# Reciprocal square roots of a four-layer decoder trunk: one GpSimd power in place of ten VectorE instructions

## The chip, the cores and the metric

One core of one Trainium2 chip runs the whole kernel in a single launch. The metric is the device time of that launch in microseconds (us). The core has TensorE (PE in the profile, its weight loads PEld), VectorE (DVE), ScalarE (ACT), GpSimd (POOL) and SyncE (SP, which here only issues DMAs). Each engine works through its own instruction queue in order, and engines wait for each other by semaphores.

## The reference

The kernel computes four decoder layers over 1024 positions of width 1024, in float32. Layers 0 and 3 mix tokens with HGRN2 (a gated linear recurrence), layer 1 with sliding-window attention, layer 2 with a gated DeltaNet. Reciprocal square roots occur in every norm:

```python
def rmsnorm(x, g):
    xf = x.astype(jnp.float32)
    y = xf * lax.rsqrt(jnp.mean(xf * xf, axis=-1, keepdims=True) + EPS)
    return (y * g.astype(jnp.float32)).astype(x.dtype)

def l2norm(x):
    xf = x.astype(jnp.float32)
    return xf * lax.rsqrt(jnp.sum(xf * xf, axis=-1, keepdims=True) + EPS)

for i in range(DEPTH):                                   # DEPTH = 4
    shift, scale, gate = jnp.split(c @ ada_w[i] + ada_b[i], 3, axis=-1)
    h = rmsnorm(x, norm_g[i]) * (1.0 + scale) + shift
    kind = i % 3
    if kind == 0:   y = hgrn2_mixer(h, ...)   # o = rmsnorm(o, onorm_g) per head
    elif kind == 1: y = swa_mixer(h, ...)     # q, k = rope(rmsnorm(q), rmsnorm(k)) per head
    else:           y = gdn_mixer(h, ...)     # q, k = l2norm(q), l2norm(k); o = rmsnorm(o) per head
    x = x + gate * y
```

## The kernel before

Activations lie with the model dimension on the 128 partitions, in two halves of 512 positions. A projection is a product of float32 values split into a high and a low part, so each 128x512 step is three matmuls (`mm3`, lines 218 to 220). Weights come from HBM by SP's queue (`w_raw`), ACT rounds them to the high part (`w_hi`, line 189) and DVE subtracts to get the low part (`w_lo`, line 190).

Inside a layer, Python generators are woven together: the token mixing of one head (`mix` in HGRN2 and attention; `inverse` and `scan` in DeltaNet) is interleaved with the projections of the next head and with the conditioning (`ada`) of the next layer. The weaving gives each instruction a priority; a scheduler then fixes the order in every engine's queue before the run, by these priorities and by its own costs for the instructions. So a change of one instruction can change the order of others.

`rsqrt` (line 164) is called at 74 places, on a small tile of mean squares (4, 8 or 16 columns by 128 partitions). It guesses from the bits of the float (line 169) and makes three Newton steps of three instructions each (lines 171 to 173): ten DVE instructions, each of which needs the one before it. The calls are:

| caller | tile | columns | calls | who reads the result |
|---|---|---|---|---|
| `norm_stats`, the pre-norm at a layer's start | `n_ms` | 4 | 8 | DVE line 519, then PE line 521 (`n_rb`), on which all of the layer's input hangs |
| HGRN2 `mix`, output norm of a head's half | `hg_ms` | 4 | 32 | DVE line 1213 (or 1221 for the last head), which empties the PSUM tile `o_ps` |
| attention `ev_k` | `k_ms` | 16 | 2 | DVE line 1404 |
| attention `proj_q` | `q_ms` | 16 | 8 | DVE line 1478 and ACT line 1485, much later |
| DeltaNet `proj_kq` | `gd_ms` | 16 | 8 | DVE lines 751 to 756, then ACT |
| DeltaNet `finish` | `gd_oms` | 8 | 16 | DVE line 909, then line 913 |

POOL has little to do before the change: in DeltaNet it fills and copies small pieces (`gd_xs`, `gd_halo`, `gd_Tb`, `gd_Z`, `gd_uq`), which the causal convolution (DVE line 690) and the block inverse (DVE lines 837 and 838, PE lines 866 to 891) need; between layers it issues the DMAs that store `x` (line 142).

Of the kernel before, what the change touches and what calls it, by code (L numbers as in the profile page):

```python
# [10 lines left out]
F32 = mybir.dt.float32  # L11
F32R = mybir.dt.float32r
BF16 = mybir.dt.bfloat16
I32 = mybir.dt.int32
U8 = mybir.dt.uint8
AF = mybir.ActivationFunctionType
ALU = mybir.AluOpType
# [3 lines left out]
P = 128  # L21
# [3 lines left out]
HT = 512  # L25
NC = HT // P
EPS = 1e-6
RSQRT_MAGIC = float(0x5F3759DF)

RAW, WB = 3, 4  # L30
NB = {"n_acc": 1, "n_sq": 2}
# [50 lines left out]
class Trunk:  # L82
# [80 lines left out]

    def rsqrt(self, x, n, tag, pool=None):

        nc, pool = self.nc, pool or self.sm
        y = pool.tile([P, n], F32, name="rs_y", tag=tag + "y", bufs=2)
        t = pool.tile([P, n], F32, name="rs_t", tag=tag + "t", bufs=2)
        nc.vector.tensor_scalar(y.bitcast(I32), x.bitcast(I32), -0.5, RSQRT_MAGIC, ALU.mult, ALU.add)
        for _ in range(3):  # L170
            nc.vector.scalar_tensor_tensor(t, y, -0.5, x, ALU.mult, ALU.mult)
            nc.vector.tensor_tensor(t, t, y, ALU.mult)
            nc.vector.scalar_tensor_tensor(y, t, 1.5, y, ALU.add, ALU.mult)
        return y

    def load_w(self, src, scale=None, pool=None):
# [46 lines left out]
    def setup(self, tmp):  # L223
        nc, const, ins = self.nc, self.const, self.ins
        self.ident = const.tile([P, P], F32, name="ident")
        make_identity(nc, self.ident)
        self.ones = const.tile([P, P], F32, name="ones")
        nc.vector.memset(self.ones, 1.0)
        self.mod = const.tile([P, 4, 24], F32, name="mod")

        rows = tmp.tile([96, P], F32, name="rows")
        nc.sync.dma_start(rows[0:32, :], ins["norm_g"].rearrange("l (k p) -> (l k) p", p=P))
        nc.sync.dma_start(rows[32:64, :], ins["hgrn_lb"].rearrange("l (k p) -> (l k) p", p=P))
        nc.sync.dma_start(rows[64:72, :], ins["c"].rearrange("o (k p) -> (o k) p", p=P))
        nc.sync.dma_start(rows[72:74, :], ins["hg_onorm"])
        nc.sync.dma_start(rows[74:75, :], ins["gd_onorm"])
        brows = tmp.tile([96, P], F32, name="brows")
        nc.sync.dma_start(brows, ins["ada_b"].rearrange("l (k p) -> (l k) p", p=P))
        self.par = const.tile([P, 96], F32, name="par")
        pt = self.psum("tr", "par_ps", 1)  # L240
        nc.tensor.transpose(pt[:, :75], rows[:75, :], self.ident[:75, :75])
        nc.tensor.transpose(pt[:, 128:224], brows, self.ident[:96, :96])
        nc.vector.tensor_copy(self.par[:, :75], pt[:, :75])
        self.adab = const.tile([P, 96], F32, name="adab")
        nc.vector.tensor_copy(self.adab, pt[:, 128:224])
        self.cT = self.par[:, 64:72]
        self.gcol = const.tile([P, 4, 8], F32, name="gcol")

        lb = self.par[:, 32:64].rearrange("p (l k) -> p l k", l=4)
        m = tmp.tile([P, 8], F32, name="lb_m")  # L250
        e = tmp.tile([P, 4, 8], F32, name="lb_e")
        s = tmp.tile([P, 8], F32, name="lb_s")
        nc.vector.tensor_tensor(m, lb[:, 0, :], lb[:, 1, :], ALU.max)
        nc.vector.tensor_tensor(m, m, lb[:, 2, :], ALU.max)
        nc.vector.tensor_tensor(m, m, lb[:, 3, :], ALU.max)
        for l in range(4):
            nc.vector.tensor_tensor(e[:, l, :], lb[:, l, :], m, ALU.subtract)
        nc.scalar.activation(e, e, AF.Exp)
        nc.vector.tensor_tensor(s, e[:, 0, :], e[:, 1, :], ALU.add)
        nc.vector.tensor_tensor(s, s, e[:, 2, :], ALU.add)  # L260
        nc.vector.tensor_tensor(s, s, e[:, 3, :], ALU.add)
        nc.vector.reciprocal(s, s)
        for l in range(4):
            nc.vector.tensor_tensor(e[:, l, :], e[:, l, :], s, ALU.mult)
        self.lb = const.tile([P, 8], F32, name="lb")
        nc.vector.tensor_tensor(self.lb, e[:, 0, :], e[:, 1, :], ALU.add)
        nc.vector.tensor_tensor(self.lb, self.lb, e[:, 2, :], ALU.add)
        nc.vector.tensor_tensor(self.lb, self.lb, e[:, 3, :], ALU.add)
        nc.vector.tensor_tensor(self.lb, self.lb, e[:, 0, :], ALU.subtract)
        self.omlb = const.tile([P, 8], F32, name="omlb")  # L270
        nc.vector.tensor_scalar(self.omlb, self.lb, -1.0, 1.0, ALU.mult, ALU.add)
# [1368 lines left out]
```

## Time and profile before

| quantity | value |
|---|---|
| median of 3 runs | 2658.29 us (2656.97 to 2660.67) |
| span of the profiled execution, first to last instruction | 2664.1 us |
| busy TensorE / VectorE / ScalarE / GpSimd | 2568.7 / 2021.6 / 1323.5 / 105.7 us |
| mean granted TensorE clock | 0.990 |

The page gives the profiled execution's span but no separate total for it; the span stands 5.8 us (0.2%) above the median of the runs. Busy time of PE is the time in which at least one matmul is under way: matmuls overlap, so their durations add up to more than that. The chain of work that ended last is followed back from the last instruction; a place on it is one where the profile saw no other instruction finish later.

### The profile page before, as it was taken

Reading aid. Unit: us, or ns where it says so; the run is one execution under the profiler, and the core shown is the slowest. Engines: PE = TensorE matmul, PEld = TensorE weight load, DVE = VectorE, ACT = ScalarE, POOL = GpSimd, SP = SyncE. Lnnn points to the kernel's source line nnn. Section 1 sums busy time; section 2 is a strip of 40 time slices with the busy share of each in tenths; the row PEclk is TensorE's granted clock in tenths of the full one; section 3 lists DMA queues with packets and bytes.
Section 4 is the critical chain, followed back from the end, with each engine's and each line's share of the span. In section 5 each row is a group of like instructions: output and inputs, shape, how many; then the busy total and the mean of one; then the engine's idle time right before and its main releaser. Section 6 shows DMA issues by size and latency. Waiting matters only on the chain.

```text
span 2664.1 us, 50723 instructions
## 1 busy us (share of the span) xinstructions
PE 2568.7 (96%) x18271; PEld 2046.2 (77%) x18271; DVE 2021.6 (76%) x5655; ACT 1323.5 (50%) x3467; POOL 105.7 (4%) x278
## 2 busy tenths in 40 slices
PE   7999999999999999999999999999999999999998
PEld 4777777778888877677877777778688877787777
DVE  5585788687697877768899999988776837368675
ACT  4443444443464655545666666666544534345352
POOL 0001000001000000101000100110000000000000
PEclk8999999999999999999999999999999999999999
DMA  7333343544233253334343444333576412122343
GB/s 261 98 114 90 116 143 115 173 128 129 67 103 104 72 160 112 95 110 111 106 123 84 118 118 119 83 97 93 174 235 188 123 48 77 42 82 64 124 139 116
DMA packets 395025, 309.96 MB, mean 116 GB/s; under 512 B 74851, under 2 KB 314902, under 8 KB 394774
## 3 DMA queue, kind: packets, MB, share of 16 engines
q1 hardware_dynamic: 390550, 293.09, 37.4%
q0 software_dynamic: 4224, 13.64, 1.6%
q8 instruction: 144, 2.36, 0.4%
q14 instruction: 107, 0.88, 0.1%
HBM read 245.75 MB, written 60.88 MB: 115 GB/s over the span
## 4 chain that ended last, share of the span: by engine, by line
PE 72%; DVE 14%; DMA 6%; ACT 5%; issue 2%; SPq 1%; DVEq 0%; ACTq 0%
PE proj_ps L218 10%; PE proj_ps L220 10%; PE proj_ps L219 10%; PE outp_ps L218 4%; PE outp_ps L219 4%; PE outp_ps L220 4%; PE projw_ps L219 2%; PE projw_ps L218 2%; PE projw_ps L220 2%; DVE gd_tb L690 1%; DVE w_lo L190 1%; PE projt_ps L219 1%; PE projt_ps L220 1%; PE pv_ps L1502 1%; PE projt_ps L218 1%
## 5 line engine op out<-in xcount | busy, mean ns | idle before, releaser
L218 PE MATMUL proj_ps<-hhi,w_hi 128*128 128x512 f32 x1664 | 676.0, 407 | 3.7 <-ACT gd_tb L688 3.3
L219 PE MATMUL proj_ps<-hlo,w_hi 128*128 128x512 f32 x1664 | 671.4, 404 | 0.0
L220 PE MATMUL proj_ps<-hhi,w_lo 128*128 128x512 f32 x1664 | 671.1, 403 | 0.0
L218 PEld LDWEIGHTS proj_ps<-hhi,w_hi 128*128 128x128 f32 x1664 | 314.6, 189 | 64.3 <-ACT gd_tb L688 5.9
L220 PEld LDWEIGHTS proj_ps<-hhi,w_lo 128*128 128x128 f32 x1664 | 314.1, 189 | 58.1 <-issue 0.4
L219 PEld LDWEIGHTS proj_ps<-hlo,w_hi 128*128 128x128 f32 x1664 | 314.6, 189 | 55.2 <-issue 0.9
L189 ACT CAST w_hi<-w_raw 128x512 fp32r<-128x512 f32 x352 | 214.5, 612 | 270.5 <-PE proj_ps L219 150.8
L190 DVE TENSOR_TENSOR w_lo<-w_raw,w_hi 128x512 fp32r<-128x512 f32 x352 | 236.5, 676 | 138.2 <-ACT w_hi L189 135.2
L218 PE MATMUL outp_ps<-o_hi,w_hi 128*128 128x512 f32 x576 | 229.8, 401 | 7.9 <-ACT o_hi L1314 7.0
L219 PE MATMUL outp_ps<-o_lo,w_hi 128*128 128x512 f32 x576 | 229.6, 399 | 0.4 <-DVE o_lo L1315 0.2
L220 PE MATMUL outp_ps<-o_hi,w_lo 128*128 128x512 f32 x576 | 228.0, 398 | 0.5 <-DVE w_lo L193 0.4
L192 ACT ACTIVATE w_hi<-w_raw,par 128x512 fp32r<-128x512 f32 (+1 forms) x136 | 94.8, 698 | 131.0 <-PE outp_ps L219 88.1
L690 DVE SCALAR_TENSOR_TENSOR gd_tb<-gd_xs,taps,gd_tb 128x512 f32<-128x512 f32 x192 | 145.7, 759 | 16.2 <-ACT gd_tb L688 12.5
L218 PEld LDWEIGHTS outp_ps<-o_hi,w_hi 128*128 128x128 f32 x576 | 109.4, 190 | 31.8 <-ACT o_hi L1314 9.7
L193 DVE SCALAR_TENSOR_TENSOR w_lo<-w_raw,par,w_hi 128x512 fp32r<-128x512 f32 (+1 forms) x136 | 96.9, 715 | 45.2 <-ACT w_hi L192 43.9
L444 DVE SCALAR_TENSOR_TENSOR ada_acc<-ada_w,par,ada_acc 128x512 f32<-128x512 f32 x154 | 114.9, 746 | 19.8 <-DMA ada_w<-in_ada_w_dram 18.8
L219 PEld LDWEIGHTS outp_ps<-o_lo,w_hi 128*128 128x128 f32 x576 | 109.4, 190 | 24.9 <-DVE o_lo L1315 3.0
L220 PEld LDWEIGHTS outp_ps<-o_hi,w_lo 128*128 128x128 f32 x576 | 109.1, 190 | 22.6 <-DVE w_lo L193 1.1
L219 PE MATMUL projt_ps<-w_lo,hhi 128*128 128x256 f32 x384 | 111.6, 292 | 2.2 <-DVE w_lo L190 2.2
L218 PE MATMUL projt_ps<-w_hi,hhi 128*128 128x256 f32 x384 | 111.0, 292 | 2.7 <-ACT w_hi L189 2.7
L220 PE MATMUL projt_ps<-w_hi,hlo 128*128 128x256 f32 x384 | 111.4, 292 | 0.0
L218 PE MATMUL projw_ps<-w_hi,hhi 128*128 128x512 f32 x256 | 102.8, 407 | 2.3 <-DVE hg_q L1032 2.3
(409 smaller groups left out, 5218.0 us busy)
## 6 DMA issues: line engine op xcount, KB each, us to landing
ada_w<-in_ada_w_dram SPq DMA_DIRECT2D x160, 256.0 KB, 2.8
w_raw<-in_hg_in_w_dram SPq DMA_DIRECT2D x136, 256.0 KB, 2.9
w_raw<-in_gd_in_w_dram SPq DMA_DIRECT2D x128, 256.0 KB, 3.0
o_in<-od SPq DMA_DIRECT2D x72, 256.0 KB, 3.7
x<-xd SPq DMA_DIRECT2D x64, 256.0 KB, 4.4
w_raw<-in_gd_out_w_dram SPq DMA_DIRECT2D x64, 256.0 KB, 3.1
xd<-x POOLq DMA_DIRECT2D x48, 256.0 KB, 2.9
w_raw<-in_sw_in_w_dram SPq DMA_DIRECT2D x48, 256.0 KB, 3.1
```

What stands on the lines that cost most here:

```text
L189: nc.scalar.copy(hi, raw)
L190: nc.vector.tensor_tensor(lo, raw, hi.bitcast(F32), ALU.subtract)
L192: nc.scalar.activation(hi, raw, AF.Copy, scale=scale)
L193: nc.vector.scalar_tensor_tensor(lo, raw, scale, hi.bitcast(F32), ALU.mult, ALU.subtract)
L218: mm(out, a[0], b[0], start=start, stop=False)
L219: mm(out, a[0], b[1], start=False, stop=False)
L220: mm(out, a[1], b[0], start=False, stop=stop)
L444: self.step = self.nc.vector.scalar_tensor_tensor(acc, w, c, acc, ALU.mult, ALU.add)
L690: last = nc.vector.scalar_tensor_tensor(y, xs[:, j:j + HT], w(j), y, ALU.mult, ALU.add)
L1502: self.tied([lambda b=b, a=a: nc.tensor.matmul(po[a * 64:(a + 1) * 64], vg[:, n + 1 - nkb + b, :], p4s[b][:, :, a, :], start=b == nkb - 1, ...
```

## The change

`rsqrt` becomes one elementwise power on GpSimd: the tile of mean squares to the power of a constant tile `mhalf`, which holds -0.5 and is written once at the start. The ten DVE instructions and the scratch tile `rs_t` are gone. The line numbers shift: the power is line 166, and what stood behind `setup`'s first lines stands 5 lines earlier (line 1213 is now 1208).

```diff
@@ -25,7 +25,6 @@
-RSQRT_MAGIC = float(0x5F3759DF)
@@ -163,14 +162,8 @@
     def rsqrt(self, x, n, tag, pool=None):
 
-        nc, pool = self.nc, pool or self.sm
-        y = pool.tile([P, n], F32, name="rs_y", tag=tag + "y", bufs=2)
-        t = pool.tile([P, n], F32, name="rs_t", tag=tag + "t", bufs=2)
-        nc.vector.tensor_scalar(y.bitcast(I32), x.bitcast(I32), -0.5, RSQRT_MAGIC, ALU.mult, ALU.add)
-        for _ in range(3):
-            nc.vector.scalar_tensor_tensor(t, y, -0.5, x, ALU.mult, ALU.mult)
-            nc.vector.tensor_tensor(t, t, y, ALU.mult)
-            nc.vector.scalar_tensor_tensor(y, t, 1.5, y, ALU.add, ALU.mult)
+        y = (pool or self.sm).tile([P, n], F32, name="rs_y", tag=tag + "y", bufs=2)
+        self.nc.gpsimd.tensor_tensor(y, x, self.mhalf[:, :n], ALU.pow)
         return y
@@ -226,6 +219,8 @@
         nc.vector.memset(self.ones, 1.0)
+        self.mhalf = const.tile([P, 16], F32, name="mhalf")
+        nc.gpsimd.memset(self.mhalf, -0.5)
```

The queues after the change hold 740 DVE instructions fewer, 74 powers and one memset more on POOL, and two ACT table loads more; PE and SP hold the same instructions. The scheduler's order differs elsewhere too: some 1,095 of PE's 14,360 entries stand at another place.

VectorE in the last layer, second half of the first HGRN2 head (`hg_ssq` are the sums of squares, `hg_tmp` the normed output, `hg_f` the next head's gates). Before:

```order
L1208 TENSOR_SCALAR hg_ms<-hg_ssq 128x4
L169 TENSOR_SCALAR rs_y<-hg_ms 128x4
L171 SCALAR_TENSOR_TENSOR rs_t<-rs_y,hg_ms 128x4
L172 TENSOR_TENSOR rs_t<-rs_t,rs_y 128x4
L173 SCALAR_TENSOR_TENSOR rs_y<-rs_t,rs_y 128x4
L171 SCALAR_TENSOR_TENSOR rs_t<-rs_y,hg_ms 128x4
L172 TENSOR_TENSOR rs_t<-rs_t,rs_y 128x4
L173 SCALAR_TENSOR_TENSOR rs_y<-rs_t,rs_y 128x4
L171 SCALAR_TENSOR_TENSOR rs_t<-rs_y,hg_ms 128x4
L172 TENSOR_TENSOR rs_t<-rs_t,rs_y 128x4
L173 SCALAR_TENSOR_TENSOR rs_y<-rs_t,rs_y 128x4
L1213 TENSOR_TENSOR hg_tmp<-o_ps,rs_y 128x4x4x32
```

The same place after:

```order
L1198 SCALAR_TENSOR_TENSOR hg_S<-hg_S,hg_F,s_ps 128x128
L1203 TENSOR_SCALAR hg_ms<-hg_ssq 128x4
L1208 TENSOR_TENSOR hg_tmp<-o_ps,rs_y 128x4x4x32
L1210 STREAM_TRANSPOSE hg_tmp<-hg_tmp 128x512
L1035 TENSOR_SCALAR hg_f<-hg_f,omlb,lb 128x512
```

The reader of the result (line 1213 before, 1208 after) now stands directly behind the instruction that makes `hg_ms`, with nothing between them while the power runs on the other engine.

VectorE in DeltaNet, `finish` of the second unit's second half, where the triangular inverse (`gd_Tb`, `gd_tmp`) of the next unit runs beside it. Before:

```order
L907 TENSOR_SCALAR gd_oms<-gd_oms 128x8
L905 TENSOR_TENSOR gd_s_17368<-gd_sc 128x4
L838 TENSOR_TENSOR gd_Tb<-gd_Tb,gd_tmp 128x4x14
L169 TENSOR_SCALAR rs_y<-gd_oms 128x8
L190 TENSOR_TENSOR w_lo<-w_raw,w_hi 128x512
L837 TENSOR_TENSOR gd_tmp<-gd_A,gd_Tb 128x45
L697 SCALAR_TENSOR_TENSOR gd_q<-gd_tb 128x512
L838 TENSOR_TENSOR gd_Tb<-gd_Tb,gd_tmp 128x3x15
L171 SCALAR_TENSOR_TENSOR rs_t<-rs_y,gd_oms 128x8
L837 TENSOR_TENSOR gd_tmp<-gd_A,gd_Tb 128x30
L172 TENSOR_TENSOR rs_t<-rs_t,rs_y 128x8
```

After:

```order
L832 TENSOR_TENSOR gd_tmp<-gd_A,gd_Tb 128x56
L902 TENSOR_SCALAR gd_oms<-gd_oms 128x8
L439 SCALAR_TENSOR_TENSOR ada_acc<-ada_w,par,ada_acc 128x512
L833 TENSOR_TENSOR gd_Tb<-gd_Tb,gd_tmp 128x4x14
L904 SCALAR_TENSOR_TENSOR gd_f<-rs_y,gd_sc 128x8
L692 SCALAR_TENSOR_TENSOR gd_q<-gd_tb 128x512
```

The ten instructions were spread between others; now two instructions (lines 439 and 833) stand between `gd_oms` and the first reader of the power (line 904).

GpSimd in DeltaNet, the stretch of its queue in the same unit. Before:

```order
L680 COPY gd_xs<-gd_halo 128x3
L828 MEMSET gd_Tb 128x512
L829 MEMSET gd_Tb 64x16
L830 MEMSET gd_Tb 64x16
L678 MEMSET gd_xs 128x3
L687 COPY gd_halo<-gd_xs 128x3
```

After:

```order
L675 COPY gd_xs<-gd_halo 128x3
L166 TENSOR_TENSOR rs_y<-gd_oms,mhalf 128x8
L166 TENSOR_TENSOR rs_y<-gd_ms,mhalf 128x16
L673 MEMSET gd_xs 128x3
L823 MEMSET gd_Tb 128x512
L824 MEMSET gd_Tb 64x16
L825 MEMSET gd_Tb 64x16
L682 COPY gd_halo<-gd_xs 128x3
```

The fills and copies for the next convolution and inverse now stand behind two powers, which wait for DVE.

Over all 74 places, the number of DVE instructions between the maker of the mean squares and the first DVE reader of the power is 0 for 18 of the 32 HGRN2 calls and 1 or 2 for the other 14; at least 1 for 20 of the 24 DeltaNet calls, and at most 2; 0 to 4 for the pre-norm; 1 or 2 for `k_ms`; and 29 to 164 for `q_ms`.

## The prediction

> **What bounds the kernel now.** I read the page's totals first, then the chain of work that ended last, then TensorE's timeline, and then asked where the ten instructions stand on that chain.
>
> ```profile
> span 2664.1 us, 50723 instructions
> PE 2568.7 (96%) x18271; PEld 2046.2 (77%) x18271; DVE 2021.6 (76%) x5655; ACT 1323.5 (50%) x3467; POOL 105.7 (4%) x278
> PE 72%; DVE 14%; DMA 6%; ACT 5%; issue 2%; SPq 1%; DVEq 0%; ACTq 0%
> ```
>
> ```profile
> 2200.06 0.39 PE L219 MATMUL proj_ps<-hlo,w_hi 128*128 128x512 f32 x1
> 2200.28 0.39 PE L220 MATMUL proj_ps<-hhi,w_lo 128*128 128x512 f32 x1
> ```
>
> TensorE is busy for 2568.7 of 2664.1 us and carries 72% of the chain. Successive matmuls start 0.22 us apart, closer than one lasts: in such a stretch PE is limited by its own rate. What a relief of VectorE can win is PE's idle time, 2664.1 - 2568.7 = 95.4 us in all, and only the part of it that waits on VectorE behind a reciprocal square root.
>
> **What the change removes.** VectorE's busy time over the span at lines 169, 171, 172 and 173, one row each:
>
> ```profile
> 0.00:2664.00 2664.00, 12.26 (x74) 0.99 0.39 116
> ...
> 0.00:2664.00 2664.00, 36.90 (x222) 0.99 0.39 116
> ...
> 0.00:2664.00 2664.00, 36.77 (x222) 0.99 0.39 116
> ...
> 0.00:2664.00 2664.00, 36.16 (x222) 0.99 0.39 116
> ```
>
> That is 740 instructions and 12.26 + 36.90 + 36.77 + 36.16 = 122.1 us of VectorE. Where nothing else fills the gaps, one call looks like this on VectorE's timeline:
>
> ```profile
> 2473.45 0.17 DVE L169 TENSOR_SCALAR rs_y<-hg_ms 128x4 int32<-128x4 int32 x1
> 2473.66 0.16 DVE L171 SCALAR_TENSOR_TENSOR rs_t<-rs_y,hg_ms 128x4 f32<-128x4 f32 x1
> ...
> 2475.23 0.16 DVE L173 SCALAR_TENSOR_TENSOR rs_y<-rs_t,rs_y 128x4 f32<-128x4 f32 x1
> 2475.44 0.69 DVE L1213 TENSOR_TENSOR hg_tmp<-o_ps,rs_y 128x512 f32<-128x512 f32 x1
> ```
>
> From 2473.45 to 2475.44 the reader waits 2.0 us. Where other work fills the gaps, a call costs nearer its own ten instructions: 122.1 / 74 = 1.65 us of busy time at most, part of it overlapped.
>
> How much of this lies on the path? In the chain of work that ended last (start, length, what), the first and the last piece at these four lines are
>
> ```profile
> 52.60 0.07 DVE rs_t L171
> ...
> 2598.91 0.07 DVE rs_y L173
> ```
>
> Added up, there are 225 such pieces with 32.2 us, against 740 instructions and 122.1 us: about three quarters of the removed time lies off the path. 30.0 of the 32.2 us stand in 19 places. Busy time per engine in the 12 us from each of them (PE, PEld, DVE, ACT, POOL; then clock, DMA share, GB/s), four of the rows and the sum:
>
> ```profile
> 142.00:154.00 12.00, 12.00 (x66) 9.75 (x60) 9.10 (x27) 4.15 (x9) 0.00 (x0) 1.00 0.49 139
> ...
> 624.00:636.00 12.00, 9.97 (x76) 9.08 (x75) 7.68 (x20) 4.50 (x9) 0.00 (x0) 1.00 0.22 66
> ...
> 1422.00:1434.00 12.00, 10.88 (x51) 8.46 (x51) 11.83 (x47) 6.24 (x20) 1.06 (x5) 1.00 0.40 83
> ...
> 2208.00:2220.00 12.00, 11.28 (x139) 8.83 (x138) 11.33 (x43) 5.33 (x11) 0.00 (x0) 1.00 0.16 45
> ...
> sum 228.00, PE 214.56 PEld 169.64 DVE 200.28 ACT 97.55 POOL 20.77; mean PE 11.29 PEld 8.93 DVE 10.54 ACT 5.13 POOL 1.09
> ```
>
> The sum is the ceiling: PE is idle for 228.00 - 214.56 = 13.4 us behind all these places. At 142 it is not idle at all, although the chain runs through VectorE there: a call can be on the chain while PE has other matmuls in its queue, and then its removal wins nothing.
>
> **What it adds.** 74 powers and one memset on GpSimd, and two handovers for each: VectorE to GpSimd and back. The handovers can be read off:
>
> ```profile
> 1256.09 0.70 DVE L850 STREAM_TRANSPOSE gd_Uc<-gd_Tc 128x512 f32<-128x512 f32 x1
> ...
> 1256.85 1.66 POOL L870 COPY gd_uq<-gd_Uc 32x512 f32<-32x512 f32 x2 [1.23 <-DVE gd_Uc L850]
> ```
>
> GpSimd starts 0.06 us after VectorE ended (1256.79 to 1256.85). I take 0.1 us for both ways. The power itself does not occur in the trace. The nearest rows on GpSimd:
>
> ```profile
> L680 POOL COPY gd_xs<-gd_halo x32: 185/186/1635, 1117.9 to 1891.8; 128x3 f32<-128x3 f32 x32
> ...
> L886 POOL COPY gd_uq<-gd_Uc x16: 602/950/1143, 1258.6 to 1875.6; 32x512 f32<-32x512 f32 x16
> ```
>
> The lower bound is the 128x3 copy at its fastest, 0.185 us; a power of 4 to 16 columns with two inputs will not beat it. The upper bound by these rows is the same copy at its slowest, 1.635 us, though no row bounds the arithmetic of a power. I take estimates between: 0.6 us for 4 columns (three times the copy, for a second input and real arithmetic), 0.8 for 8 and 1.2 for 16 (about the longest of the 512-element copies).
>
> The Trainium skill ("GPSIMD Engine Reference", section "Performance versus the Vector engine") speaks against the change in general: VectorE is about twice as fast for elementwise work. By its 2.6 cycles per element at 1.2 GHz, 4 columns would add an estimated 0.01 us to the fixed cost; with the copy's 0.185 us as the fixed cost that is the lower bound's sum below. It gives no price for a power, and no run here shows one yet.
>
> **The sum.** At each of the 19 places the path time of the call is replaced by a round trip of 0.7 us (4 columns: eleven HGRN2 calls, one pre-norm), 0.9 (8 columns) or 1.3 (16 columns; five places in DeltaNet hold nine calls of both kinds, two are `k_ms`). Together 12 x 0.7 + 2 x 1.3 + 5 x 0.9 + 4 x 1.3 = 20.7 us, against 30.0: the path is shorter by 9.3 us. Taking at each place the smaller of the saving and PE's idle time there (1.0 at 624, 0.7 at 2208, 0.3 at 1422, nothing at 142 and so on), 6 us are left. With 0.185 us per power the same sum gives 11 us, close under the ceiling of 13.4. With 1.635 us it gives a loss of 10 us: a standalone call breaks even (2.0 against 1.74), but the DeltaNet places, where two calls together take 1.9 to 2.7 us of path, lose about 1 us each.
>
> Costed at nothing: the removed 92 us off the path (covered by PE's own queue); the eight `q_ms` powers (29 or more VectorE instructions stand before the first reader); the memset (at the start, where PE waits for DMAs); and two more ACT table loads,
>
> ```profile
> L1029 ACT ACT_TABLE_LOAD x3 | 3.8, 1283 | 0.1
> ```
>
> 2.6 us of an engine that is busy half the time; if one of them lands on the path it costs its 1.3 us. GpSimd's `x` stores between layers stand in front of the pre-norm's power, but their last source is ready before the mean squares are summed. The other entries that move in PE's queue I put at 0, with 5 us either way. Behind the waiting reader on VectorE stand the low parts of the weights (line 190) and the next head's gates; behind the waiting power on GpSimd the convolution's `gd_xs` and `gd_halo`.
>
> The forecast is -6 us on the span of 2664.1 us. The median of the runs stands 0.2% below that span, which does not change a difference of this size: 2658.3 - 6 = 2652. A measurement of this kernel can tell about 0.2%, 5.3 us, from no change.
>
> **Rivals.**
>
> *The power is long (slower).* VectorE waits at 66 of 74 places with at most four instructions in between. DeltaNet is where it has least room (columns as above):
>
> ```profile
> 1190.00:1300.00 110.00, 106.61 (x717) 86.32 (x716) 91.71 (x249) 61.10 (x175) 9.08 (x23) 1.00 0.46 121
> ...
> sum 770.00, PE 747.67 PEld 597.18 DVE 684.21 ACT 481.63 POOL 62.21; mean PE 249.22 PEld 199.06 DVE 228.07 ACT 160.54 POOL 20.74
> ```
>
> From 1190 to 1960 VectorE is busy for 684 of 770 us, 86 us free. Of its 24 calls there, the nine on the chain take 10.1 us of it, 1.1 us each. At 4 us for 8 and 16 columns (4.1 with the handovers), VectorE would lose 24 x 3.0 = 72 us, nearly all of its room; with an estimated half of that reaching PE, the time is 2658 + 36 = 2694, and HGRN2's longer waits would add to it: 2700. It decides from about 1 us per power in DeltaNet and 1.9 elsewhere. Against it: no GpSimd row of that length; for it: no row with arithmetic of that kind.
>
> *Each blocks the other at SBUF (slightly slower).* The 128x3 copy usually takes 0.186 us, once 1.635. Then VectorE was running, among others,
>
> ```profile
> 1510.85 1.64 POOL L680 COPY gd_xs<-gd_halo 128x3 f32<-128x3 f32 x1 [1.96 <-DVE gd_tmp L837]
> ...
> 1510.84 0.74 DVE L444 SCALAR_TENSOR_TENSOR ada_acc<-ada_w,par,ada_acc 128x512 f32<-128x512 f32 x1
> ```
>
> Two large SBUF inputs, started together with GpSimd's copy. If every such instruction between maker and reader (20 places in DeltaNet, 14 in HGRN2, about 0.7 us each) holds the power back, 34 x 0.7 = 24 us of VectorE waiting come on top; half of it on the path gives -6 + 12 = +6, 2664 to 2665. The Trainium skill ("SBUF — State Buffer", section "Who interferes with whom") has this as a rule: a VectorE instruction with two SBUF inputs contends with a GpSimd one that reads SBUF, and the later one blocks. The trace agrees in that one row; the copies' median of 0.186 us says that it is rare.
>
> *PE hides it (same).* PE's own rate takes up the saving, as at 142, or the power costs 1 to 1.5 us: within 5 us of 2658.
>
> **How the numbers follow.** Forecast, 2652, with gains of 5.3 us or more: 0.42. Hidden or break-even, 2658: 0.25. Long power, 2700 or more: 0.22. Blocking, 2665: 0.11. Hence faster 0.42, same 0.25, slower 0.33. The range goes from 2642 (the 11 us of the lower bound with the 5 us of reordering) to 2715 (the long power at 4 us, and half as much again of its loss in HGRN2): below it 0.05, above it 0.15, where a power of ten or more us would lie. The forecast's own range is 2642 to 2656.
>
> **What would show it.** VectorE's busy time near 1900 us. The power's rows: 0.6 to 1.2 us mean confirm the price. VectorE's idle time before lines 1208, 904, 746 and 514, released by the power, should be 0.5 to 1 us a time; if it is above 1.9 us, or above 1 us in DeltaNet, the forecast is wrong. PE's idle time should fall by about 6 us, behind the places named; a copy or a power whose longest case is over 1.5 us shows blocking. The windows of the HGRN2 layers should get shorter even where DeltaNet does not.

## The result, and the profile after

| quantity | before | after |
|---|---|---|
| median of the four runs of each, side by side | 2659.11 us (2656.97 to 2660.67) | 2728.12 us (2726.59 to 2735.64) |
| ratio after to before, 95% interval | | 1.0255 (1.0239 to 1.0271) |
| span of the profiled execution | 2664.1 us | 2724.8 us |
| TensorE idle, span less busy | 95.4 us | 144.1 us |

The kernel became slower by about 68 us (0.0255 x 2659). The forecast was 2652, 7 us faster, and the time lies above the upper end of its range, 2715. The totals of the page after the change, and the shares by engine of the chain that ended last:

```profile
span 2724.8 us, 50129 instructions
...
PE 2580.7 (95%) x18271; PEld 2053.3 (75%) x18271; DVE 1941.7 (71%) x4915; ACT 1326.6 (49%) x3469; POOL 229.9 (8%) x353
...
PE 66%; DVE 16%; ACT 6%; DMA 5%; issue 3%; POOL 3%; SPq 1%; POOLq 0%; DVEq 0%; ACTq 0%
```

VectorE did lose its work: 79.9 us less busy. But the span grew by 60.7 us, and this splits into 48.7 us more idle time of TensorE and 12.0 us more busy time (2580.7 against 2568.7) for the same 18271 matmuls. GpSimd, busy for 8% of the span, now stands on the chain with 3% of it. The power's own rows (shortest, median and longest in ns, then first and last start, then the shape) and those who waited for it (us, times):

```profile
L166 POOL TENSOR_TENSOR rs_y<-hg_ms,mhalf x32: 1006/1007/1185, 145.1 to 2657.9; 128x4 f32<-128x4 f32 x32
L166 POOL TENSOR_TENSOR rs_y<-gd_oms,mhalf x16: 1631/1639/2117, 1310.9 to 2005.3; 128x8 f32<-128x8 f32 x16
L166 POOL TENSOR_TENSOR rs_y<-n_ms,mhalf x8: 1032/1058/1453, 13.6 to 2161.5; 128x4 f32<-128x4 f32 x8
L166 POOL TENSOR_TENSOR rs_y<-q_ms,mhalf x8: 2900/3294/3810, 663.3 to 955.3; 128x16 f32<-128x16 f32 x8
L166 POOL TENSOR_TENSOR rs_y<-gd_ms,mhalf x8: 2894/3067/3424, 1198.9 to 1840.6; 128x16 f32<-128x16 f32 x8
...
  DVE hg_tmp L1208: 28.5, 27
  DVE gd_f L904: 25.1, 16
  DVE gd_ir L746: 23.0, 8
  DVE n_sq L514: 6.5, 7
  DVE sw_tmp L1399: 5.0, 2
  DVE hg_tmp L1216: 4.7, 4
```

Three things stand in these rows. The power's price goes with the columns: 1.0 us for 4, 1.64 for 8, 2.9 or more for 16. VectorE stood still for it 64 times, 92.8 us in all. And the eight `q_ms`, the group with the longest powers (up to 3.8 us), are not among those waited for.

Where the time went by layer: DeltaNet's stretch, from the third layer's pre-norm to the fourth's first, in both kernels. The columns are the length, then busy time of PE, PEld, DVE, ACT and POOL with their instructions, the granted clock, DMA share and GB/s.

```profile
1109.20:2059.10 949.90, 924.46 (x6078) 738.89 (x6078) 803.89 (x2138) 561.13 (x1649) 69.94 (x179) 1.00 0.46 125
```

```profile
1119.70:2112.70 993.00, 935.35 (x6074) 749.25 (x6074) 779.11 (x1888) 560.20 (x1648) 121.58 (x208) 0.98 0.44 120
```

The second row is the kernel after. DeltaNet took 43.1 us longer: TensorE idle 57.7 us instead of 25.4, and 10.9 us longer busy for the same matmuls, at a granted clock of 0.98 instead of 1.00. Most of the rest lies in layer 0 (HGRN2), whose end came 12 us later.

How one such wait works is seen on the timeline. DeltaNet's second `gd_ms` after the change (start, length, what, and in brackets the idle time before it and who ended it):

```profile
1276.29 0.17 DVE L739 TENSOR_SCALAR gd_ms<-gd_ms 128x16 f32<-128x16 f32 x1 [0.60 <-ACT gd_tb L705]
1276.61 2.91 POOL L166 TENSOR_TENSOR rs_y<-gd_ms,mhalf 128x16 f32<-128x16 f32 x1 [4.16 <-DVE gd_ms L739]
...
1277.05 0.40 PE L212 MATMUL proj_ps<-hlo,w_hi 128*128 128x512 f32 x1
...
1279.55 0.17 DVE L746 TENSOR_TENSOR gd_ir<-gd_ms,rs_y 128x8 f32<-128x8 f32 x1 [3.09 <-POOL rs_y L166]
...
1279.91 0.68 DVE L883 COPY gd_Z<-z_ps 64x512 f32<-64x512 f32 x1
...
1280.74 1.97 PE L886 MATMUL z_ps<-gd_uq,gd_Z 64*64 64x64 f32 x32 [3.29 <-DVE gd_Z L883]
```

The same place before:

```profile
1264.57 0.17 DVE L169 TENSOR_SCALAR rs_y<-gd_ms 128x16 int32<-128x16 int32 x1
1265.43 0.69 DVE L888 COPY gd_Z<-z_ps 64x512 f32<-64x512 f32 x1
1266.15 0.18 DVE L171 SCALAR_TENSOR_TENSOR rs_t<-rs_y,gd_ms 128x16 f32<-128x16 f32 x1
...
1266.27 1.15 PE L891 MATMUL z_ps<-gd_uq,gd_Z 64*64 64x64 f32 x32 [0.47 <-DVE gd_Z L888]
```

TensorE does not wait for the square root at all. It waits for `gd_Z`, a copy that has nothing to do with it and stands behind the reader in VectorE's queue. Before, that copy slipped in between the guess and the first Newton step, and TensorE waited 0.47 us. Now it is held back with the reader, and TensorE waits 3.29 us.

Behind that wait the matmuls are slow (the 32 small ones at 1280.74 took 1.97 us, before 1.15): two windows of 7 us, around the wait and after it.

```profile
1273.00:1280.00 7.00, 3.61 (x42) 2.46 (x40) 3.22 (x9) 4.80 (x16) 2.91 (x1) 1.00 0.26 75
1280.00:1287.00 7.00, 6.26 (x49) 5.88 (x50) 4.87 (x13) 1.49 (x3) 0.00 (x0) 0.55 0.41 117
```

The granted clock (third number from the right) falls from 1.00 to 0.55. By the granted clock over time, TensorE ran at half clock for 34 us of DeltaNet after the change, which is up to 17.1 us of lost work, in eight places; six of them begin 4 to 8 us behind the start of a `gd_ms` power, two 3 and 7 us behind a `gd_oms` power. Before it lost 1.7 us, in one place.

In HGRN2 the same happens on a smaller scale. Layer 3, first half of a head, before:

```profile
2412.22 0.17 DVE L1208 TENSOR_SCALAR hg_ms<-hg_ssq 128x4 f32<-128x4 f32 x1
...
2412.46 0.16 DVE L169 TENSOR_SCALAR rs_y<-hg_ms 128x4 int32<-128x4 int32 x1
2412.53 0.18 DVE L1177 TENSOR_TENSOR hg_F<-hg_F 128x16 f32<-128x16 f32 x1
...
2413.44 0.28 DVE L1139 TENSOR_TENSOR hg_X<-hg_X,hg_F 128x128 f32<-128x128 f32 x1
...
2414.24 0.65 PE L1161 MATMUL lev_ps<-hg_X,hg_kg 128*32 128x32 f32 x32
```

and after (the power began at 2470.07):

```profile
2469.75 0.17 DVE L1203 TENSOR_SCALAR hg_ms<-hg_ssq 128x4 f32<-128x4 f32 x1
...
2471.11 0.69 DVE L1208 TENSOR_TENSOR hg_tmp<-o_ps,rs_y 128x512 f32<-128x512 f32 x1 [0.99 <-POOL rs_y L166]
...
2474.35 0.28 DVE L1134 TENSOR_TENSOR hg_X<-hg_X,hg_F 128x128 f32<-128x128 f32 x1
...
2474.78 0.65 PE L1156 MATMUL lev_ps<-hg_X,hg_kg 128*32 128x32 f32 x32 [0.68 <-DVE hg_F L1167]
```

Before, a Newton instruction between two others took 0.07 us of the queue (2412.46 to 2412.53), the level product's input `hg_X` came 1.2 us behind `hg_ms`, and TensorE did not wait. After, `hg_X` came 4.6 us behind `hg_ms` and 3.2 us behind the waiting reader, and TensorE waited 0.68 us. The order of VectorE's queue differs between the two as well, so these lines show where the wait falls and not what it costs; the pairs of kernels below do that.

### The profile page after: what moved, and what is told of

It reads as the page before. It is cut to its first block, busy times and chain, and to the rows that moved or that the text cites. A ratio compares the mean times of both kernels' runs of the same rounds, so it can differ in the third digit from the quotient of the medians.

```text
span 2724.8 us, 50129 instructions
## 1 busy us (share of the span) xinstructions
PE 2580.7 (95%) x18271; PEld 2053.3 (75%) x18271; DVE 1941.7 (71%) x4915; ACT 1326.6 (49%) x3469; POOL 229.9 (8%) x353
## 4 chain that ended last, share of the span: by engine, by line
PE 66%; DVE 16%; ACT 6%; DMA 5%; issue 3%; POOL 3%; SPq 1%; POOLq 0%; DVEq 0%; ACTq 0%
PE proj_ps L212 9%; PE proj_ps L211 9%; PE proj_ps L213 9%; PE outp_ps L212 4%; PE outp_ps L211 4%; PE outp_ps L213 4%; POOL rs_y L166 3%; PE projw_ps L212 2%; PE projw_ps L211 2%; PE projw_ps L213 2%; DVE gd_tb L685 2%; PE projt_ps L211 1%; PE projt_ps L212 1%; PE projt_ps L213 1%; DVE w_lo L183 1%
## 5 line engine op out<-in xcount | busy, mean ns | idle before, releaser
L212 PE MATMUL proj_ps<-hlo,w_hi 128*128 128x512 f32 x1664 | 678.3, 408 | 0.0
L186 DVE SCALAR_TENSOR_TENSOR w_lo<-w_raw,par,w_hi 128x512 fp32r<-128x512 f32 (+1 forms) x136 | 96.9, 715 | 45.5 <-ACT w_hi L185 43.5
L166 POOL TENSOR_TENSOR rs_y<-hg_ms,mhalf 128x4 f32<-128x4 f32 x32 | 33.0, 1030 | 901.6 <-DVE hg_ms L1203 693.1
```

The costliest lines, as they stand in the source:

```text
L166: self.nc.gpsimd.tensor_tensor(y, x, self.mhalf[:, :n], ALU.pow)
L186: nc.vector.scalar_tensor_tensor(lo, raw, scale, hi.bitcast(F32), ALU.mult, ALU.subtract)
L212: mm(out, a[0], b[1], start=False, stop=False)
```

## Experiments

Each kernel ran beside the kernel before on the same chip. Microseconds "above" or "below" are worked out as (ratio - 1) times the median of the kernel before there: 2665.8 for `short`, `guess`, `gd_newton` and `hg_only`, 2663.5 for the `hg_late` pair, `q_only` and `newton2`, 2662.1 for `g_only`, `go_only` and the `hg_late0` pair, and 2664.4 for `hg_mult` and the `hg_both` pair.

### Length, handover or order?

Two theories for the 68 us: the power's length, or the handover between engines and the new order. `short` keeps every engine's queue as after and changes only the power into a multiply. `guess` measures what the relief of VectorE is worth without GpSimd.

```diff
# short (from the kernel after)
-        self.nc.gpsimd.tensor_tensor(y, x, self.mhalf[:, :n], ALU.pow)     # mhalf = -0.5
+        self.nc.gpsimd.tensor_tensor(y, x, self.mhalf[:, :n], ALU.mult)    # mhalf = 0.001
# guess (from the kernel before): the guess stays, the loop of Newton steps goes
-        for _ in range(3):
-            ...
```

> The change with every engine's queue in exactly its order, but the GpSimd instruction multiplies by 0.001 instead of taking the power (the norms' values are meaningless, the work is not). Theory A, the length of the power: VectorE waits in order behind it, 92.8 us in all. A multiplication should last 0.2 to 0.5 us, the waits should fall to about 20 us, the half-clock stretches in DeltaNet should go, and the time should be 2645 to 2665. Theory B, the handover or the shared SBUF path to GpSimd: the time stays above 2690. Theory C, the scheduler's other order of the queues: it stays at 2700 or more, since the order is the same.

> VectorE's guess alone, all three Newton steps left out, nothing on GpSimd (values are off by some per cent). This is what VectorE's relief is worth by itself: 666 instructions and 110 us fewer. If the prediction's ceiling holds, 2645 to 2653. If TensorE hides it, 2656 to 2661. If the order that the scheduler makes of it matters more than the relief, it can come out on either side by 10 us.

Measured: `short` 2659.93 us, ratio 0.9979 (0.9969 to 0.9989), 5.6 us below the kernel before; `guess` 2655.41, ratio 0.9965 (0.9952 to 0.9979), 9.3 us below. In `short` the multiply's row and VectorE's waits for it in HGRN2 read

```profile
L168 POOL TENSOR_TENSOR rs_y<-hg_ms,mhalf x32: 195/201/381, 147.3 to 2592.3; 128x4 f32<-128x4 f32 x32
...
  DVE hg_tmp L1219: 6.4, 20
```

against 1007 ns and 28.5 us with the power. The traces of `short` and of the kernel after have the same instructions in the same order on VectorE, ScalarE and GpSimd. So the loss is the length of the power: with the same order and the same handovers the change would have won 5.6 us (2.9 to 8.3). Handover and order are refuted as causes of the 68 us. The same holds for DeltaNet alone: between the same two pre-norms `short` took 947.1 us, with TensorE idle for 23.1 us and two places at half clock (5.1 us lost), against 993.00 us after and 949.90 us before.

The relief of VectorE is worth up to 9.3 us, inside the 6 to 13.4 us that the prediction read from the idle time behind the calls.

### Which powers?

```diff
# gd_newton, hg_only, q_only, g_only, go_only: some calls only
+        if tag in (...):   # ("n","hg","q","k"); ("hg",); ("q",); ("g",) = gd_ms; ("go",) = gd_oms
+            y = (pool or self.sm).tile([P, n], F32, name="rs_y", tag=tag + "y", bufs=2)
+            self.nc.gpsimd.tensor_tensor(y, x, self.mhalf[:, :n], ALU.pow)
+            return y
         # else the guess and three Newton steps, as before
```

> The change with DeltaNet's 24 calls back on VectorE's Newton steps. Theory A: DeltaNet grew by 45 us between the pre-norms of layers 2 and 3, which should go: 2680 to 2688. If the growth in DeltaNet came from something other than its own powers, above 2700.

> Only HGRN2's 32 calls on GpSimd. Its power took 1.0 us against 1.9 us for the ten instructions, so by the prediction's own step it should win: 2650 to 2656. By the after trace layers 0 and 3 grew by 12.7 and 5.0 us, and if that is HGRN2's powers: 2670 to 2678. If layer 0's growth came from elsewhere: about 2658 to 2664.

> Only the eight roots of the sliding-window layer's queries (q_ms, 16 columns, the power took 2.9 to 3.8 us there, the longest of all) are powers; the rest is Newton's steps as before. In the changed kernel VectorE never waited for these eight at all: their readers stand at least 29 instructions behind. Theory (the power's length matters only where the reader stands close behind): no wait on it, the same time as the kernel before to 0.2%, or up to 3 us less, since 80 VectorE instructions are gone (the run that left out 666 instructions of Newton's steps gained 10 us: 0.015 us each, so 1 us). Rival (a power disturbs the other engines while it runs, for some 25 us in all here): slower by 3 us or more although nothing waits for it.

> Only DeltaNet's eight roots of 16 columns (gd_ms, reader gd_ir) are powers; Newton everywhere else. In the changed kernel VectorE waited 23.0 us for these eight, 3.3 at the longest. Theory (VectorE stands still in its own order behind the reader, and each such wait is late for TensorE's next chunk): the time rises by about that, 15 to 25 us above the kernel before. TensorE's clock: in the changed kernel DeltaNet had eight stretches at half clock, each 8 to 20 us behind one of these eight powers, against one stretch before; if the long waits bring them, six or more stand here too, and the loss is at the upper end. Rival (the waits of DeltaNet's finish, gd_oms, carry DeltaNet's 45 us): at most 8 us above, and one or two half-clock stretches.

> Only DeltaNet's 16 roots of the finish (gd_oms, 8 columns, reader gd_f) are powers; Newton everywhere else. In the changed kernel VectorE waited 25.1 us for these, 16 times, 1.8 at the longest. Theory (every wait of VectorE's costs its length where TensorE is fed step by step): 12 to 25 us above the kernel before, and with the run that has gd_ms alone it adds up to about 40 to 46. Rival (the finish is off the path, its waits are hidden, and gd_ms carries all): within 6 us of the kernel before, with one or two stretches at half clock.

| powers in | columns | median | ratio (95%) | above before |
|---|---|---|---|---|
| all but DeltaNet (`gd_newton`) | 4, 16 | 2687.97 | 1.0085 (1.0070 to 1.0100) | 22.7 us |
| HGRN2 only (`hg_only`) | 4 | 2683.61 | 1.0071 (1.0055 to 1.0087) | 18.9 us |
| attention's queries only (`q_only`) | 16 | 2663.24 | 1.0004 (0.9995 to 1.0012) | 1 us, not told from none |
| `gd_ms` only (`g_only`) | 16 | 2695.00 | 1.0115 (1.0092 to 1.0138) | 30.6 us |
| `gd_oms` only (`go_only`) | 8 | 2682.89 | 1.0074 (1.0050 to 1.0099) | 19.7 us |

`q_only` carries the longest powers, and nobody waited for one:

```profile
L168 POOL TENSOR_TENSOR rs_y<-q_ms,mhalf x8: 2899/3279/3882, 651.5 to 938.3; 128x16 f32<-128x16 f32 x8
```

Some 26 us of power beside the other engines cost nothing that can be measured. DeltaNet's two kinds cost 50 us when tried apart; in the kernel after, DeltaNet's powers make up 45 us (68 - 23). VectorE's waits and DeltaNet's stretch in `g_only`:

```profile
DVE gd_ir L757 <- POOL rs_y L168: 21.7, 8, 3.2
...
1106.10:2086.60 980.50, 939.74 (x6078) 755.11 (x6078) 794.73 (x2058) 559.99 (x1649) 98.14 (x187) 0.97 0.44 121
```

and in `go_only`:

```profile
DVE gd_f L915 <- POOL rs_y L168: 25.2, 16, 1.8
...
1110.80:2082.30 971.50, 933.15 (x6078) 745.57 (x6078) 787.13 (x1978) 562.78 (x1649) 101.10 (x195) 0.99 0.45 122
```

`go_only` has the longer sum of waits (25.2 against 21.7 us) and loses less time (the intervals of the two ratios just meet, and its profiled execution, 2689 us, is the slowest of its four). Against the 949.90 us before, `g_only` is idle 15.3 us longer (40.8 against 25.4) and busy 15.3 us longer; its clock is 0.97, with 25.5 us lost to half clock, in ten places. `go_only` is idle 12.9 us longer and busy 8.7 us longer, with 13.6 us lost to half clock, in three. My expectation for `g_only`, 15 to 25 us, stayed under the result: it took the waits' length and not the clock on top. Of the ten half-clock stretches seven begin 3 to 10 us behind the start of a power, two 18 and 21 us behind one, and one far from any; of the three in `go_only` one begins 6 us behind a power and two 12 us or more. So not every such stretch can be put down to a power; `short` has two without a long one. The rival, that `gd_oms` carries all, is refuted, and so is the one that its waits are hidden.

The run `go_only` also bears on the prediction's rival of blocking at SBUF. Nine of its sixteen powers took 2.00 to 2.17 us, the other seven 1.64 to 1.68 us. The nine are those that began while a VectorE instruction of about 0.7 us with two SBUF inputs was already running. The first two lines are one of them; the last two, from the kernel after, show a power that began 0.08 us ahead of such an instruction:

```profile
1392.84 0.69 DVE L194 TENSOR_TENSOR w_lo<-w_raw,w_hi 128x512 fp32r<-128x512 f32 x1
1392.95 2.08 POOL L168 TENSOR_TENSOR rs_y<-gd_oms,mhalf 128x8 f32<-128x8 f32 x1
...
1407.11 1.64 POOL L166 TENSOR_TENSOR rs_y<-gd_oms,mhalf 128x8 f32<-128x8 f32 x1 [29.84 <-DVE gd_s L900]
1407.19 0.69 DVE L183 TENSOR_TENSOR w_lo<-w_raw,w_hi 128x512 fp32r<-128x512 f32 x1 [0.19 <-ACT w_hi L182]
```

VectorE's instruction lasts 0.69 us in both; the power is 0.44 us longer where it came second. Over all 74 powers of the kernel after, the time above the shortest row of the same size adds up to 9 us of 128. No run varies this alone, but by these rows blocking is there, and it is small.

Two things stay open for DeltaNet. No run moves its readers away from the powers, so that the wait in VectorE's queue is the way by which the length costs time is read from timelines there. And GpSimd's own queue is a second way: its fills and copies stand behind the powers. By the profile they ended 4.9 us of other engines' idle time in DeltaNet after the change and 2.1 us before; the longest, 3.4 us of a weight load at 1655, was over 0.7 us before VectorE had made its own copy `gd_uq`, for which the matmul waited too. That is little beside 57.7 us of idle TensorE, but no run takes it apart.

### Why do HGRN2's powers cost 19 us, at 1 us each?

`hg_only` is the run that contradicts the prediction most. By its working, 2.0 us of reader's wait were replaced by 1.1, and the layers should have become shorter. I took the urgent work behind the reader for the cause, and moved the reader in the queue (with it the gating of the finished half; the controls have both): first in the second halves of six heads a layer (`hg_late`), then in the first halves (`hg_late0`), then in both (`hg_both`).

```diff
# hg_late, hg_late0, hg_both: the reader is traced later and tied behind hg_X of the next half
-                    nc.vector.tensor_tensor(v4(on, "b c"), v4(po, "c b"), r[...], ALU.mult)
-                    ... transpose, stores, pend.append(...)
+                    late.append(fin)
 ...
+                    xl = nc.vector.tensor_tensor(xv[:, :, nx - 1, :], ...)       # last part of hg_X
+                    late.pop()(xl)     # fin: with tc.issue_after(xl.ins): the reader, and the rest
# *_newton: the same without powers.  *_mult: the same with ALU.mult, mhalf = 0.001
# hg_mult: hg_only with ALU.mult, mhalf = 0.001
```

> Only HGRN2's 32 reciprocal roots are powers on GpSimd (Newton everywhere else), as in the run that had this alone and stood 18 us above the kernel before. New: in 12 of the 32 places, the second halves of heads 1 to 6 of both layers, the reader of the root stands behind the next head's first level inputs (hg_F, hg_qf, hg_X) on VectorE, 10 to 17 instructions behind the mean of squares instead of 1 to 3; the first halves, whose reader frees the PSUM bank of the other half's output, stay as they were. Theory (what the power costs is the urgent work that stands behind the waiting reader, above all those level inputs): VectorE's wait in front of the reader falls by about 12 x 1.0 us, from 28 to about 16 us, and the time by more than half of the 18 us, to at most 9 us above the kernel with the same order and Newton's steps. Rival one (GpSimd's power costs by itself, by what it takes from VectorE's or TensorE's memory ports, wherever the reader stands): the waits fall as said, but the time stays within 4 us of 18 us above. Rival two (the first halves carry the cost): the same, with TensorE's idle time behind the first halves' readers.

> The control of the run before it: the same move of 12 readers behind the next head's level inputs, but with Newton's three steps everywhere, so no power. Newton's steps stand between other work already (11 to 26 instructions lie between the mean of squares and its reader in the kernel before), so the move should do little: all theories expect within 4 us of the kernel before. If it is itself faster or slower, the run with powers is judged against this one, not against the kernel before.

Measured: `hg_late` 2688.22, ratio 1.0094 (1.0081 to 1.0107); its control 2673.20, 1.0036 (1.0024 to 1.0049). So 15 us above the control, where I had expected at most 9, and the control is 9.6 us above the kernel before where I had expected 4. VectorE's wait fell as said, but the time did not follow. The timeline of `hg_late` says why: 

```profile
2380.51 0.17 DVE L1216 TENSOR_SCALAR hg_ms<-hg_ssq 128x4 f32<-128x4 f32 x1
...
2381.86 0.69 DVE L1221 TENSOR_TENSOR hg_tmp<-o_ps,rs_y 128x512 f32<-128x512 f32 x1 [0.96 <-POOL rs_y L168]
...
2385.73 0.48 PE L1169 MATMUL lev_ps<-hg_X,hg_kg 128*32 128x32 f32 x24 [0.66 <-DVE hg_X L1145]
```

This is a first half, whose reader I had left in place, and TensorE's wait for `hg_X` of the second half follows it. So the first halves came next.

> HGRN2's 32 roots are powers, Newton elsewhere. This time the reader of the first halves stands later: behind the second half's last level input hg_X, so 13 instructions behind the mean of squares in four heads of layer 3 instead of 3 (in layer 0 the scheduler leaves 2 to 4); the second halves' reader is where it was. In the run that moved the second halves' readers, VectorE did not wait for the power there any more, but a head of layer 3 still took 46.0 us against 45.4 with Newton in the same order, and TensorE's wait of 0.7 us on hg_X stood 4 us behind the first half's reader. Theory (what costs is hg_X and hg_F of the second half, queued behind the first half's waiting reader): a head of layer 3 is now within 0.2 us of its Newton control, and TensorE's wait of 0.7 us on hg_F or hg_X is gone from these heads; layer 0 keeps its loss. Rival (the power itself slows VectorE or TensorE): the head stays 0.5 us or more above the control.

> Control of the run before it: the same move of the first halves' readers, Newton's steps everywhere, no power. A head of layer 3 took 44.4 us in the kernel before and 45.2 to 45.5 in every version with another order of instructions (two Newton steps, the guess alone, the other move). Expected for this one: 44.4 to 45.5 a head, and within 10 us of the kernel before in all; it is the yardstick for the power with the same move.

Measured: `hg_late0` 2687.38, ratio 1.0087 (1.0064 to 1.0110); control 2668.84, 1.0017 (1.0006 to 1.0029). The move reached only four heads of layer 3, and VectorE still waited 24 times at these readers instead of 27. TensorE's 0.7 us wait was gone from layer 3's heads, but a head took 45.6 us against 44.7 with Newton's steps. By the mark I had set, the rival (the running power slows the others) had won. But these controls were not clean: without the Newton steps the scheduler orders VectorE's queue differently. A head of layer 3 took 44.5 us in the kernel before and 45.5 in `short`, where nothing is long. The last three runs therefore compare pairs with the same order in every queue.

> The run with HGRN2's 32 powers alone, instruction for instruction in the same order on every engine, with a GpSimd multiply by 0.001 (0.2 us) in the place of each power (1.01 us); so HGRN2's normalisation is left out. Theory: of the 18 us that the powers cost there, about 11 are the power's length (VectorE standing in front of the reader) and about 7 the new order that the scheduler makes once the Newton steps are gone (a head of layer 3 took 45.5 us in the all-multiply version, 44.5 before): so 4 to 10 us above the kernel before, and a head of layer 3 at 45.4 to 45.6. Rival (all 18 us are the power's length): within 3 us of the kernel before. Second rival (all of it is order and handover): 15 us or more above.

> HGRN2's 32 roots are powers, and the readers of both halves stand behind the level inputs hg_X of what comes next: 9 to 18 instructions behind the mean of squares in 20 of the 28 places of heads 0 to 6, 1 to 6 in the others. Theory (only the wait in VectorE's order costs): VectorE's wait on the power falls from 33 to about 13 us; a head of layer 3 is within 0.2 us of the same order with the multiply; in all at most 6 us above that control. Rival (a running power slows VectorE or TensorE wherever its reader stands): a head of layer 3 stays 0.5 us or more above the control and the total 9 us or more.

> Control of hg_both: the same order on every engine, with the multiply by 0.001 in the place of each power, so HGRN2's normalisation is left out. Both theories expect the new order to be worth some us by itself, 0 to 10 us above the kernel before, and a head of layer 3 at 44.4 to 46; what counts is the difference to hg_both.

Measured: `hg_mult` 2666.47, ratio 1.0004 (0.9995 to 1.0013); `hg_both` 2681.67, 1.0062 (1.0049 to 1.0075); `hg_both_mult` 2675.18, 1.0041 (1.0027 to 1.0054). Three heads of layer 3, the same three in each kernel, in the order `hg_mult`, `hg_only`, `hg_both_mult`, `hg_both` (columns as above):

```profile
2362.16:2498.52 136.36, 134.33 (x1358) 105.46 (x1357) 95.20 (x310) 60.59 (x168) 1.20 (x6) 1.00 0.24 71
```

```profile
2378.66:2517.27 138.61, 134.60 (x1358) 105.56 (x1357) 94.85 (x310) 60.61 (x168) 6.05 (x6) 1.00 0.24 70
```

```profile
2365.35:2503.14 137.79, 135.22 (x1359) 105.39 (x1358) 94.24 (x313) 60.70 (x169) 1.60 (x6) 1.00 0.24 70
```

```profile
2377.29:2515.00 137.71, 135.21 (x1359) 105.41 (x1358) 94.19 (x313) 60.64 (x169) 6.45 (x6) 1.00 0.24 70
```

With the readers in place, power for multiply lengthens three heads by 2.25 us, 0.75 a head. With the readers of both halves moved away it lengthens them by nothing (137.71 against 137.79), although GpSimd is busy for 6.45 us there instead of 1.60. So in these heads the running power does not slow the others; the standing queue behind its reader is the cost. In the whole, the power's length costs 18 us in `hg_only` (1.0071 - 1.0004, each against the kernel before on its own chip) and 6 us in `hg_both` (1.0062 - 1.0041), where VectorE still waited 13.1 us for it, 12 times, in the first heads and the last of both layers. The second is known to about 5 us only. Two of my expectations failed: I had put 7 of the 19 us down to the new order, and `hg_mult` shows about 1, what the new order costs being about what the relief wins; and moving a reader is not free (`hg_both_mult`, 11 us above the kernel before).

### Fewer Newton steps

```diff
-        for _ in range(3):
+        for _ in range(2):
```

> All roots stay on VectorE, with two Newton steps instead of three, so 222 VectorE instructions fewer (74 calls x 3). No engine is handed anything. The run that left out all three steps of every call stood about 10 us below the kernel before (666 instructions); a third of that is 3 us, if the gain goes with the number of instructions; if it sits only in the eight chains that stand alone in front of idle engines it is up to 4 us. Both theories of the power's cost expect the same here: this run is the version that may beat both kernels, and says how much of Newton's price can be had without GpSimd.

Measured: 2666.23 us, ratio 1.0007 (0.9997 to 1.0017). The 3 us were not had: a head of layer 3 took 45.2 us in it against 44.5 before, so here too the new order gives back what the relief wins. No version that keeps the whole computation beats the kernel before by more than the measurement can tell.

## Why the prediction was wrong, step by step

- **The price of the power** is the step that failed first. The estimates 0.6, 0.8 and 1.2 us were scaled from copies, and the text itself said that no row bounds the arithmetic. Measured: 1.01, 1.64 and 2.9 to 3.3 us, above the upper bound of 1.635 for 16 columns. `short`, with the price near the lower bound (0.20 us), came out 5.6 us faster. That this is the forecast's 6 is chance: for such a price the prediction's own sum gives 11.
- **Break-even per call** failed on its own. The prediction set the reader's wait after a standalone Newton chain (2.0 us) against the round trip (1.74 at the bound), and said that the power decides from 1.9 us outside DeltaNet. HGRN2's powers took 1.0 us and lost 19. What counts is not when the reader can start but what stands behind it: Newton's steps let other work pass between them for 0.07 us each, the wait lets nothing pass.
- **Off the path, so costed at nothing.** The sum was made over the 19 places that were on the chain before. Removing a call off the chain wins nothing, but the wait that replaces it can lose: VectorE waited at 64 places, 92.8 us, and `gd_ms` and `gd_oms` each lost 20 to 31 us by themselves. The order that the document shows ahead of the prediction (0 to 2 instructions between maker and reader) carried this; it was used for the rival and not for the sum.
- **TensorE's clock** was not in the sum. Of DeltaNet's 43.1 us, 10.9 are longer busy time of the same matmuls, at a lower granted clock. The Trainium skill ("TensorE: Matmul & The Clock Gate", section "Why this matters for your kernels") warns of TensorE idle gaps of more than about 3 us, behind which the clock halves; the trace agrees, with an idle of 3.29 us and a clock of 0.55 in the next 7 us. Of DeltaNet's eight half-clock stretches after the change four follow an idle time of 3.0 to 3.9 us and four a shorter one of 1.6 to 2.95 us, and the one before the change follows 1.2 us; so in this kernel staying under 3 us did not keep the clock up.
- **The relief** stayed under its ceiling of 13.4 us: 9.3 in `guess`, and 5.6 in `short`, where the sum gave 11. **Order**, put at 5 us either way, was not measured apart from the relief: the two together came out 1 us above in `hg_mult` and 5.6 below in `short`. The moved readers show that an order can cost 10.
- **The rival "the power is long"** was right in mechanism and place, and low by 28 us in its example of 2700. It had 4 us for DeltaNet's 8 and 16 columns (measured 1.64 and 3.07) and let half of VectorE's loss reach TensorE. Of the 48.1 us of waits there two thirds did, as 32.2 us of idle time, and the clock added 10.9. That its 36 us for DeltaNet lie near the measured 43 is in part luck: the price was too high and the share too low, and by its own formula the measured prices give about 13 (VectorE loses 16 x 0.64 + 8 x 2.07 = 27 us, half of it counts). The upper end of the range, 2715, is 2712 by its own terms (36 and 18 us on 2658). Its chance of 0.22 was too small for a price that nothing bounded.
- **The rival "each blocks the other at SBUF"** was right that it happens and wrong in size: in `go_only` nine of sixteen powers were 0.36 to 0.54 us longer behind a VectorE instruction with two SBUF inputs, but in all it is at most 9 us of GpSimd's time where the rival put 24 us of VectorE's waiting. The other way round, a power slowing the other engines, did not show: `hg_both`, with powers of 4 columns, equals its control in three heads of layer 3.
- **The quantities to watch** worked in DeltaNet and not in HGRN2. The waits in front of lines 904 and 746 (1.8 and 3.3 us at the longest) were above their mark of 1 us, and the 8- and 16-column powers above 1.2 us. But the 4-column powers (1.03 us on the mean) and the waits in front of line 1208 (1.2 us at the longest) were inside the marks of 1.2 and 1.9 us, while HGRN2 lost 19 us: the mark of 1.9 us came from the break-even that failed. TensorE's idle time was to fall by 6 us and rose by 48.7, and the layers of HGRN2 got longer, by 12 and 7 us. VectorE's busy time was to be near 1900 us and was 1941.7: the 122.1 us are a sum of four rows in which the time shared with neighbouring instructions is counted as well, and 79.9 us were gained.

## What to carry to other kernels

Price a handed-over operation by the queue it stops: look at what stands behind the reader on the in-order engine, not at how long the old chain took, since a chain of small dependent instructions lets other work through and a wait does not. A long operation on an idle engine is free where its reader stands far behind (`q_ms`, 29 or more instructions, 3.3 us each, no cost), and expensive where the scheduler, which orders a power as it orders a multiply (`short`), sets the reader right behind. Where no row prices the new operation, and arithmetic is involved, the case in which it is long deserves as much chance as the case in which it is cheap.

## What the hardware showed that I had not expected

- A float32 power on GpSimd costs 0.38 us and 0.157 us for each column of 128: the shortest rows are 1.006, 1.631 and 2.894 us for 4, 8 and 16 columns. A multiply of the same shapes takes 0.195, 0.199 and 0.215 us at its shortest, so nearly all of it is the power's arithmetic. The Trainium skill ("GPSIMD Engine Reference", section "Performance versus the Vector engine") counts about 2.6 cycles an element for an elementwise operation of two inputs, at 1.2 GHz; the multiply agrees with a price that columns hardly change, the power is some seventy times that per column.
- Idle time of TensorE costs more than its length in DeltaNet: in `g_only` TensorE was idle 15.3 us longer and busy 15.3 us longer with the same matmuls, in `go_only` 12.9 and 8.7 us, in the kernel after 32.2 and 10.9 us.
- The order of the kernel before is worth about 1 us a head in layer 3 by itself: 44.5 us, against 45.2 to 45.5 in four versions with fewer VectorE instructions and nothing long (`short`, `guess`, `newton2`, `hg_mult`).
